# Up and gate projections as seven half-size products instead of eight, in a three-layer network on one core

## The chip, the core and the metric

One core of a Trainium2 chip runs the whole program in one launch. The metric is the device time of an execution in microseconds (us), as the median of several runs; less is better. The engines are TensorE (PE, matmuls out of SBUF into PSUM banks), VectorE (DVE), ScalarE (ACT), GpSimd (POOL) and SyncE (SP, which here issues the DMAs).

## The reference

512 tokens of width 1024, everything in fp32. The changed part is the feed-forward work of each layer:

```python
# layers 1 and 2 (first_block): D_FF = 4096
def squared_relu_mlp(x, w_up, w_down):
    return jnp.square(jax.nn.relu(x @ w_up)) @ w_down
h = layer_norm(DN_ALPHA * h + mix, ln_mix_g[i], ln_mix_b[i])
h = layer_norm(DN_ALPHA * h + squared_relu_mlp(h, mlp_w_up[i], mlp_w_down[i]), ln_mlp_g[i], ln_mlp_b[i])
# layer 3 (second_block): FFN_HIDDEN = 2816, mod = silu(c) @ w_ada + b_ada
mod = cond @ w_ada[l] + b_ada[l]
h = modulate(rms_norm(x, norm_ffn_g[l]), sh2, sc2)
ffn = (jax.nn.silu(h @ w_gate[l]) * (h @ w_up[l])) @ w_down[l]
x = x + g2[:, None, :] * ffn
return rms_norm(x, final_norm_g)
```

Ahead of each stand a mixer and its output projection (sparse attention in layer 1, gated linear attention in layer 2, attention and mLSTM in layer 3), which the change leaves as they are.

## The kernel before

Every fp32 operand of a large product is held as two parts, hi (the value rounded to fp32r) and lo (the rest), and a product is three matmuls: hi x hi, hi x lo, lo x hi (`mm3`, line 79; every matmul of that kind is recorded at line 77). The high part is a ScalarE copy (`hi`, line 87/88), the low part a subtraction (`lo`, line 84/85).

Weights stream through three rotating pairs of buffers of 1 MB (pool `wp`, `bufs=2`): `raw` takes the DMA from SP, `wh` and `wl` its parts. `wcols` (line 122) loads, `wsplit` (line 107) splits in two pieces; VectorE makes the low part of one, GpSimd that of the other. Both run under `urgent` (line 59), which gives them a priority ahead of all other work, in their own order. The framework sorts each engine's instructions by priority and readiness ahead of time; on the chip each engine then runs its list in order.

The input of an MLP lies in SBUF as `xT_hi` and `xT_lo` (features on partitions, 8 blocks of 128 features x 512 tokens). `proj_pairs` (line 185) makes blocks of 128 hidden columns x 512 tokens: 8 feature blocks x 3 matmuls of 512 columns into a PSUM bank with the tag "a" (three of them) or "o" (one). Called with two pairs, as at the start of each MLP and of the FFN, it makes four blocks and does the first 256 tokens of all before the second 256, with 256-column matmuls, so that it can begin while the last two token tiles are still being normalised.

`mlp` (line 508) works through the 4096 hidden columns in four groups of 1024: eight hidden blocks, each evacuated by ReLU on ScalarE, a square and a low part on VectorE (`ev_up`, lines 519 to 523) into `hh` and `hl`; then the down projection with these 1024 rows, for each half of the 1024 outputs, in four token tiles of 128 (`proj_tok`, `proj_steps`, line 147; 24 matmuls of 512 columns a tile). `ev` adds each tile into `acc` on VectorE (lines 534 and 536); in the last group's second half tile after tile gets its layer norm (`ln_stats`, `ln_tile`, lines 217 to 235), whose output is transposed on TensorE (line 207) and split for the next stage. In the first MLP `ada` (line 722) is interleaved: six rows of `mod`, two after each of the first three groups, each with eight loads of 512 KB (`mod_raw`, three buffers), eight VectorE operations (lines 742 and 744) and four small matmuls into a bank "s".

`ffn` (line 1155) does the same for 22 hidden blocks in groups of 8, 8 and 6: gate block through SiLU on ScalarE, up block times it on VectorE, split; in the last group the down tiles are multiplied by `g2`, added to x, normalised and written out (lines 1204 to 1217).

## Time and profile before

| | |
|---|---|
| median of 3 runs | 1968.23 us (1962.83 to 1969.54) |
| span of the profiled execution | 1965.4 us |
| TensorE busy | 1893.6 us, 8980 matmuls |
| VectorE busy | 1101.5 us |
| ScalarE busy | 770.3 us |
| GpSimd busy | 432.6 us |
| first MLP, FFN (after their first four blocks) | 293 to 633, 1614 to 1958 us |
| second MLP (after its first four blocks) | 937 to 1260 us |

A busy time says how long an engine had an instruction in it. An engine that is busy nearly all the time in a stage is that stage's first candidate for the bound; the chain of waits, followed back from the end, says which engine's work really followed on which. In the list of instructions a matmul's own duration includes its run through the array, which overlaps with the next one; what a matmul costs in a stream is the distance from start to start. The clock that TensorE was granted is given in tenths or hundredths of 2.4 GHz. All durations below come from the one profiled execution, whose time is its span.

### The profile page before, as it was taken

Reading aid. Unit: us, or ns where it says so; the run is one execution under the profiler, and the core shown is the slowest. Engines: PE = TensorE matmul, PEld = TensorE weight load, DVE = VectorE, ACT = ScalarE, POOL = GpSimd, SP = SyncE. Lnnn points to the kernel's source line nnn. Section 1 sums busy time; section 2 is a strip of 40 time slices with the busy share of each in tenths; the row PEclk is TensorE's granted clock in tenths of the full one; section 3 lists DMA queues with packets and bytes.
Section 4 is the critical chain, followed back from the end, with each engine's and each line's share of the span. In section 5 each row is a group of like instructions: output and inputs, shape, how many; then the busy total and the mean of one; then the engine's idle time right before and its main releaser. Section 6 shows DMA issues by size and latency. Waiting matters only on the chain.

```text
span 1965.4 us, 23252 instructions
## 1 busy us (share of the span) xinstructions
PE 1893.6 (96%) x8980; PEld 1506.7 (77%) x8980; DVE 1101.5 (56%) x1866; ACT 770.3 (39%) x1378; POOL 432.6 (22%) x221
## 2 busy tenths in 40 slices
PE   8999999999999999999999999999999899999998
PEld 7865688777878788778888888777666688888886
DVE  4997575657465478556533434668875762223235
ACT  5578532223232443422322323235667442223133
POOL 2121122222221212111222222312103221122621
PEclk9999999999999999999999999999999999999999
DMA  4222144556442311124233223222112132232322
GB/s 135 86 51 79 52 154 160 174 193 215 133 144 84 98 44 57 61 84 129 94 100 106 86 86 107 85 65 95 43 22 81 43 102 91 86 108 86 103 79 75
DMA packets 126106, 190.58 MB, mean 97 GB/s; under 512 B 8239, under 2 KB 76795, under 8 KB 125996
## 3 DMA queue, kind: packets, MB, share of 16 engines
q1 hardware_dynamic: 125956, 189.03, 29.8%
q8 instruction: 71, 1.16, 0.2%
q14 instruction: 39, 0.32, 0.1%
q0 software_dynamic: 32, 0.07, 0.0%
q10 hardware_dynamic: 8, 0.00, 0.0%
HBM read 186.95 MB, written 2.12 MB: 96 GB/s over the span
## 4 chain that ended last, share of the span: by engine, by line
PE 80%; DVE 11%; issue 3%; ACT 2%; DMA 2%; POOL 0%; SPq 0%; DVEq 0%; ACTq 0%; POOLq 0%
PE ps_a L77 66%; PE ps_o L77 4%; DMA mod_raw<-in_w_ada_dram 2%; PE ps_s L77 2%; DVE wl L85 2%; PE ps_t L347 2%; PE ps_t L207 1%; PE ps_s L639 1%; DVE mod_acc L744 1%; PE ps_a L1095 1%; PE ps_t L310 1%; DVE x_tok L232 1%; DVE sc L426 1%; PE ps_s L1061 1%; ACT wh L88 1%
## 5 line engine op out<-in xcount | busy, mean ns | idle before, releaser
L85 POOL TENSOR_TENSOR wl<-wr,wh 128x1024 fp32r<-128x1024 f32 (+3 forms) x145 | 368.0, 2540 | 1309.5 <-ACT wh L88 1204.1
L88 ACT ACTIVATE wh<-wr 128x1024 fp32r<-128x1024 f32 (+2 forms) x290 | 283.5, 1025 | 503.0 <-PE ps_a L77 400.2
L77 PE MATMUL ps_a<-xT_hi,wh 128*128 128x512 f32 (+1 forms) x1056 | 402.1, 381 | 0.0
L77 PE MATMUL ps_a<-xT_lo,wh 128*128 128x512 f32 (+1 forms) x1056 | 401.2, 380 | 0.0
L77 PE MATMUL ps_a<-xT_hi,wl 128*128 128x512 f32 (+1 forms) x1056 | 401.2, 380 | 0.0
L85 DVE TENSOR_TENSOR wl<-wr,wh 128x1024 fp32r<-128x1024 f32 (+3 forms) x145 | 183.1, 1263 | 328.2 <-ACT wh L88 324.9
L77 PE MATMUL ps_a<-wh,hh 128*128 128x512 f32 x688 | 269.1, 391 | 0.4 <-ACT hh L88 0.4
L77 PE MATMUL ps_a<-wh,hl 128*128 128x512 f32 x688 | 268.9, 391 | 0.2 <-DVE hl L85 0.2
L77 PEld LDWEIGHTS ps_a<-xT_hi,wh 128*128 128x128 f32 x1056 | 202.4, 192 | 41.4 <-ACT wh L88 1.2
L77 PEld LDWEIGHTS ps_a<-xT_lo,wh 128*128 128x128 f32 x1056 | 202.5, 192 | 40.4 <-issue 1.6
L77 PEld LDWEIGHTS ps_a<-xT_hi,wl 128*128 128x128 f32 x1056 | 202.1, 191 | 40.1 <-issue 0.8
L77 PE MATMUL ps_a<-wh,xT_hi 128*128 128x512 f32 (+3 forms) x536 | 208.1, 393 | 1.9 <-ACT xT_hi L88 1.9
L77 PE MATMUL ps_a<-wh,xT_lo 128*128 128x512 f32 (+3 forms) x536 | 207.4, 390 | 0.5 <-DVE xT_lo L85 0.5
L77 PE MATMUL ps_a<-wl,hh 128*128 128x512 f32 x688 | 186.1, 391 | 0.0
L77 PEld LDWEIGHTS ps_a<-wh,hh 128*128 128x128 f32 x688 | 129.2, 188 | 28.7 <-ACT hh L88 0.8
L77 PEld LDWEIGHTS ps_a<-wh,hl 128*128 128x128 f32 x688 | 129.2, 188 | 28.4 <-DVE hl L85 0.5
L77 PEld LDWEIGHTS ps_a<-wl,hh 128*128 128x128 f32 x688 | 129.0, 188 | 27.8
L77 PE MATMUL ps_a<-wl,xT_hi 128*128 128x512 f32 (+3 forms) x536 | 147.7, 386 | 0.0
L77 PEld LDWEIGHTS ps_a<-wh,xT_lo 128*128 128x128 f32 x536 | 103.4, 193 | 20.8 <-issue 1.6
L77 PEld LDWEIGHTS ps_a<-wh,xT_hi 128*128 128x128 f32 x536 | 103.5, 193 | 20.1 <-ACT xT_hi L88 2.2
L77 PEld LDWEIGHTS ps_a<-wl,xT_hi 128*128 128x128 f32 x536 | 96.4, 190 | 18.1 <-issue 0.8
L522 DVE TENSOR_TENSOR relu<-relu 128x512 f32<-128x512 f32 x64 | 87.8, 1375 | 25.2 <-ACT relu L521 25.2
(368 smaller groups left out, 2314.8 us busy)
## 6 DMA issues: line engine op xcount, KB each, us to landing
wr<-in_mlp_w_up_dram SPq DMA_DIRECT2D x32, 1024.0 KB
wr<-in_mlp_w_down_dram SPq DMA_DIRECT2D x32, 1024.0 KB
mod_raw<-in_w_ada_dram SPq DMA_DIRECT2D x48, 512.0 KB
wr<-in_b_w_in_dram SPq DMA_DIRECT2D x12, 1024.0 KB
wr<-in_w_gate_dram SPq DMA_DIRECT2D x11, 1024.0 KB
wr<-in_w_up_dram SPq DMA_DIRECT2D x11, 1024.0 KB
wr<-in_w_in_dram SPq DMA_DIRECT2D x10, 1024.0 KB
wr<-in_w_down_dram SPq DMA_DIRECT2D x10, 1024.0 KB
```

The source lines that it names most:

```text
L77: self.nc.tensor.matmul(ps, lt, rt, start=first, stop=last)
L85: (eng or self.nc.vector).tensor_tensor(out, x, hi.bitcast(F32), op=ALU.subtract)
L88: self.nc.scalar.activation(out, x, AF.Copy)
L207: self.nc.tensor.transpose(ps[:, j * P : (j + 1) * P], src[:, j * P : (j + 1) * P], self.ident)
L232: nc.vector.scalar_tensor_tensor(x, x, rs, b[:, sl], op0=ALU.mult, op1=ALU.add)
L310: nc.tensor.transpose(ps[:, j * P : (j + 1) * P], st[:, j0 + j, :], net.identr)
L347: nc.tensor.transpose(pst[:, kb * P : (kb + 1) * P], pr[:, kb * P : (kb + 1) * P], net.ident)
L426: nc.vector.scalar_tensor_tensor(sc, rl, iws[:, t, h : h + 1], sc, op0=ALU.mult, op1=ALU.add)
L522: nc.vector.tensor_tensor(r, r, r, op=ALU.mult)
L639: nc.tensor.matmul(ps[:, c * 64 : c * 64 + 64], x[:, c * C : (c + 1) * C], xv[:, c * m : (c + 1) * m, 1, :], start=True, stop=True)
L744: nc.vector.scalar_tensor_tensor(acc, raw, cd[:, k : k + 1], acc, op0=ALU.mult, op1=ALU.add)
L1061: nc.tensor.matmul(ps, qk[:, 4 + h, a * P : (a + 1) * P], qk[:, h, :], start=True, stop=True)
```

## The change

The up projection of a 256-column chunk is seen as a 2 x 2 block product: the weight chunk [1024, 256] as four quarters (two halves of the rows, two blocks of 128 columns), the input as four quarters (two halves of the features, two halves of the tokens). In Strassen's form (with the sums as Winograd arranged them) seven products of quarters do what eight did, with sums of quarters taken before and after:

- `x_sums`, once for an MLP or the FFN, makes four sums of input quarters and splits each into `th` and `tl`, on VectorE and ScalarE. Its scratch tiles have the tags "eo" (two buffers) and "eu".
- `w_sums` takes the place of `wsplit` for these chunks: parts of three raw quarters into `wh` and `wl`, four sums in place, parts of the four sums into `wsh` and `wsl` (three buffers each, two used by a chunk). All low parts and sums are VectorE's, GpSimd takes none.
- `proj_seven` runs the seven products, each of 4 feature blocks x 3 matmuls of 256 columns, two products to a PSUM bank ("aaao", all four), and combines them on VectorE into `eo`.
- The down projection takes 512 rows at a time (`down_half`) and stands between the up chunks: chunk 2g, down of group g-1, chunk 2g+1. Its tiles use the banks "s" and "t" in turn, one tile after the other.
- The first two chunks of an MLP (the first of gate and of up in the FFN) stay as one proj_pairs call with 256-column matmuls.
- In the MLPs the square moves from VectorE to ScalarE, down tiles are added into x itself, the norm's rows are loaded into the buffers of `th` and `tl` at the end; `ada` gives one row after each of six groups, with two buffers for `mod_raw`; in the FFN all scaling by `g2` moves to the last group.

The rest of the diff removes comments. Its core:

```diff
+    def x_sums(self, pool):
+        th = pool.tile([P, 4, 4, S // 2], F32R, tag="th", name="th")
+        tl = pool.tile([P, 4, 4, S // 2], F32R, tag="tl", name="tl")
+        q = lambda x, k, t: x[:, 4 * k : 4 * k + 4, t * (S // 2) : (t + 1) * (S // 2)].bitcast(F32)
+        h, l = lambda k, t: q(self.xh, k, t), lambda k, t: q(self.xl, k, t)
+        tt = nc.vector.tensor_tensor
+        tmp = pool.tile([P, 4, S // 2], F32, name="eu")
+        f3, f1 = (pool.tile([P, 4, S // 2], F32, tag="eo", name="xsum", bufs=2) for _ in range(2))
+        for f, a, b in ((f3, (1, 1), (0, 1)), (f1, (0, 0), (0, 1))):
+            tt(f, h(*a), h(*b), op=ALU.subtract)
+            tt(tmp, l(*a), l(*b), op=ALU.subtract)
+            tt(f, f, tmp, op=ALU.add)
+        self.split(th[:, 0], tl[:, 0], f1)
+        self.split(th[:, 2], tl[:, 2], f3)
+        tt(f3, f3, h(0, 0), op=ALU.add)
+        tt(f3, f3, l(0, 0), op=ALU.add)
+        nc.scalar.activation(th[:, 1], f3, AF.Copy, scale=-1.0)
+        nc.vector.scalar_tensor_tensor(tl[:, 1], f3, -1.0, th[:, 1].bitcast(F32), op0=ALU.mult, op1=ALU.subtract)
+        tt(f3, f3, h(1, 0), op=ALU.subtract)
+        tt(f3, f3, l(1, 0), op=ALU.subtract)
+        self.split(th[:, 3], tl[:, 3], f3)
+    def w_sums(self, pool, w, c0):
...
+            a11, a21, a12, a22 = v[:, 0, :, 0], v[:, 0, :, 1], v[:, 1, :, 0], v[:, 1, :, 1]
+            self.hi(q4(wh[:, 0:512]), a11)
+            self.hi(wh[:, 512:1536], raw[:, 1024:2048])
+            self.lo(q4(wl[:, 0:512]), a11, q4(wh[:, 0:512]))
+            self.lo(wl[:, 512:1536], raw[:, 1024:2048], wh[:, 512:1536])
+            tt(a22, a22, a21, op=ALU.add)
+            tt(a21, a21, a11, op=ALU.add)
+            tt(a11, a11, a22, op=ALU.add)
+            tt(a12, a12, a11, op=ALU.add)
+            for i in range(2):
+                self.hi(sh[i], v[:, i])
+                self.lo(sl[i], v[:, i], sh[i])
...
+    def proj_seven(self, pool, w, c0, xs):
...
+        b0, b1, b2, b3 = (self.bank(x) for x in "aaao")
+        prods = [("A11", raw(0, 0), b0[:, :H]), ("A12", raw(1, 0), b1[:, :H]), ("A22", ts(3), b3[:, H:]),
+                 ("S2", ts(1), b1[:, H:]), ("S1", ts(0), b2[:, :H]), ("S3", ts(2), b2[:, H:]), ("S4", raw(1, 1), b3[:, :H])]
+        for name, (xh, xl), ps in prods:
+            wh, wl = ws[name]
+            for k in range(4):
+                self.mm(ps, wh[:, k], xh[:, k], k == 0, False)
+                self.mm(ps, wh[:, k], xl[:, k], False, False)
+            for k in range(4):
+                self.mm(ps, wl[:, k], xh[:, k], False, k == 3)
+            if name == "A11":
+                nc.scalar.activation(eu[:, 3], ps, AF.Copy)
+            elif name == "S2":
+                tt(eo[:, 0], eu[:, 3], b1[:, :H], op=ALU.add)
+                tt(eu[:, 0], eu[:, 3], b1[:, H:], op=ALU.add)
+            elif name == "S3":
+                tt(eu[:, 1:3], eu[:, 0:1].to_broadcast([P, 2, H]), two(b2), op=ALU.add)
+                tt(eo[:, 3], eu[:, 2], b2[:, :H], op=ALU.add)
+        tt(eo[:, 1:3], eu[:, 1:3], two(b3), op=ALU.add)
 def mlp(net, i, extra=None, parts=True, after=None):
...
+        def up(c):
+            e = net.proj_seven(mp, w_up, c * 256, xs)
+            hh, hl = hidden()
+            for h in range(2):
+                v = e[:, 2 * h : 2 * h + 2]
+                nc.scalar.activation(v, v, AF.Relu, scale=1.0 - 2.0 * h)
+            nc.scalar.activation(e, e, AF.Square)
+            v = e.rearrange("p (f t) n -> p f (t n)", f=2)
+            net.split(hh, hl, v)
...
+        net.proj_pairs([(w_up, 2 * i * P, lambda b, ps, i=i: ev_up(2 * i + b, ps)) for i in range(2)])
+        for g in range(1, NG + 1):
+            if g < NG:
+                up(2 * g)
...
             for n in range(2):
+                down_half(net, w_dn, g - 1, n, hid, ev_dn)
+            if g < NG:
+                up(2 * g + 1)
+            if extra is not None and g <= 6:
+                extra[g - 1](mp)
 def ffn(net):
...
+        def up(c):
+            sg = net.proj_seven(fp, wg, c * 256, xs)
+            for h in range(2):
+                v = sg[:, 2 * h : 2 * h + 2]
+                nc.scalar.activation(v, v, AF.Silu, scale=1.0 - 2.0 * h)
+            e = net.proj_seven(fp, wu, c * 256, xs)
+            hh, hl = hidden()
+            nc.vector.tensor_tensor(e[:, 0:2], e[:, 0:2], sg[:, 0:2], op=ALU.mult)
+            nc.vector.scalar_tensor_tensor(e[:, 2:4], e[:, 2:4], -1.0, sg[:, 2:4], op0=ALU.mult, op1=ALU.mult)
+            net.split(hh, hl, e.rearrange("p (f t) n -> p f (t n)", f=2))
...
+        net.proj_pairs([(wg, 0, ev_g), (wu, 0, ev_u)])
+        up(1)
+        for g in range(1, NG + 1):
+            if g < NG:
+                up(2 * g)
...
             for n in range(2):
+                down_half(net, wd, g - 1, n, hid, ev_dn)
+            if 2 * g + 1 < NCH:
+                up(2 * g + 1)
```

In `mlp` NG is 8, so chunks 2 to 15 go through `proj_seven`; in `ffn` NCH is 11 and NG 6, so chunks 1 to 10, gate and up each.

## Rows read from the trace of the kernel before

**Rows 1.** The page's first part: busy time, share of the span and instructions of each engine.
```profile
PE 1893.6 (96%) x8980; PEld 1506.7 (77%) x8980; DVE 1101.5 (56%) x1866; ACT 770.3 (39%) x1378; POOL 432.6 (22%) x221
```

**Rows 2.** Busy time by stretch (first MLP, second MLP, FFN, each after its first four blocks): start and end, length, busy time and count of PE, PEld, DVE, ACT, POOL, granted clock, DMA share, GB/s.
```profile
293.00:633.00 340.00, 334.39 (x1469) 267.57 (x1468) 195.94 (x191) 93.97 (x121) 76.59 (x30) 0.99 0.48 160
...
937.00:1260.00 323.00, 323.00 (x1397) 262.38 (x1396) 131.86 (x133) 94.62 (x124) 73.36 (x29) 1.00 0.31 98
...
1614.00:1958.00 344.00, 343.95 (x1485) 278.91 (x1484) 108.03 (x112) 96.63 (x132) 96.03 (x47) 1.00 0.28 92
```

**Rows 3.** The chain that ended last, in order of time: start, length, what, number of instructions. The first row lies in the 256-column matmuls of the FFN's first pairs; the two others are 512-column streams of the second MLP and of the FFN.
```profile
936.97 322.24 PE ps_a L77 x1392
...
1601.89 8.55 PE ps_a L77 x72
...
1613.28 344.69 PE ps_a L77 x1488
```

**Rows 4.** Instructions in order of time in the FFN, by engine (VectorE, ScalarE, GpSimd): start, duration, engine, line, operation, count, idle time before.
```profile
1702.79 1.22 DVE L85 TENSOR_TENSOR wl<-wr,wh 128x1024 fp32r<-128x1024 f32 x1 [4.21 <-ACT wh L88]
...
1701.69 2.01 ACT L88 ACTIVATE wh<-wr 128x1024 fp32r<-128x1024 f32 x2 [1.26 <-PE ps_a L77]
...
1703.84 2.42 POOL L85 TENSOR_TENSOR wl<-wr,wh 128x1024 fp32r<-128x1024 f32 x1 [3.01 <-ACT wh L88]
```

**Rows 5.** Groups of instructions in the first MLP (293 to 633 us), VectorE and ScalarE, shapes kept apart: count, busy us, mean ns of one, idle before.
```profile
L744 DVE SCALAR_TENSOR_TENSOR mod_acc<-mod_raw,cond,mod_acc 128x1024 f32<-128x1024 f32 x39 | 58.4, 1498 | 10.0 <-DMA mod_raw<-in_w_ada_dram 9.5
...
L536 DVE TENSOR_TENSOR acc<-acc,ps_a 128x512 f32<-128x512 f32 x22 | 15.1, 688 | 46.8 <-PE ps_a L77 46.8
...
L756 DVE TENSOR_TENSOR mod_row<-ps_s,mod_b 128x256 f32<-128x256 f32 x6 | 2.5, 420 | 0.4 <-PE ps_s L77 0.4
...
L88 ACT ACTIVATE hh<-relu 128x512 fp32r<-128x512 f32 x29 | 18.3, 632 | 77.7 <-DVE relu L522 77.7
L521 ACT ACTIVATE relu<-ps_a 128x512 f32<-128x512 f32 x28 | 16.3, 583 | 15.9 <-PE ps_a L77 15.7
```

**Rows 6.** VectorE in order of time: the last low parts of xT ahead of the first MLP, the second MLP and the FFN.
```profile
276.32 1.37 DVE L85 TENSOR_TENSOR xT_lo<-ps_t,xT_hi 128x512 fp32r<-128x512 f32 x2 [1.85 <-ACT xT_hi L88]
...
920.47 1.36 DVE L85 TENSOR_TENSOR xT_lo<-ps_t,xT_hi 128x512 fp32r<-128x512 f32 x2 [2.20 <-ACT xT_hi L88]
...
1599.59 0.69 DVE L85 TENSOR_TENSOR xT_lo<-ps_t,xT_hi 128x512 fp32r<-128x512 f32 x1 [0.58 <-ACT xT_hi L88]
```

**Rows 7.** The chain that ended last: the last of the four first blocks (bank "o") in the first MLP, the second MLP and the FFN.
```profile
289.98 2.85 PE ps_o L77 x24
...
934.12 2.85 PE ps_o L77 x24
...
1610.43 2.85 PE ps_o L77 x24
```

**Rows 8.** TensorE's matmuls in order of time around 263 to 271 us, the start of the first MLP.
```profile
262.66 0.28 PE L77 MATMUL ps_a<-xT_hi,wl 128*128 128x256 f32 x1
...
265.08 0.36 PE L77 MATMUL ps_a<-xT_hi,wh 128*128 128x256 f32 x1
...
268.56 0.41 PE L77 MATMUL ps_a<-xT_hi,wl 128*128 128x256 f32 x1
...
268.78 0.41 PE L77 MATMUL ps_a<-xT_hi,wh 128*128 128x256 f32 x1
...
270.91 0.32 PE L77 MATMUL ps_a<-xT_lo,wh 128*128 128x256 f32 x1
...
271.07 0.28 PE L77 MATMUL ps_a<-xT_hi,wl 128*128 128x256 f32 x1
...
271.19 0.28 PE L77 MATMUL ps_a<-xT_hi,wh 128*128 128x256 f32 x1
```

**Rows 9.** VectorE in order of time at the end of the first MLP (first operation of each of the four last token tiles, then the last operation) and of the second (first and last).
```profile
622.08 0.69 DVE L536 TENSOR_TENSOR acc<-acc,ps_a 128x512 f32<-128x512 f32 x1 [3.07 <-PE ps_a L77]
...
628.93 0.68 DVE L536 TENSOR_TENSOR acc<-acc,ps_a 128x512 f32<-128x512 f32 x1
...
635.47 0.68 DVE L536 TENSOR_TENSOR acc<-acc,ps_a 128x512 f32<-128x512 f32 x1
...
647.76 0.68 DVE L536 TENSOR_TENSOR acc<-acc,ps_a 128x512 f32<-128x512 f32 x1
...
654.69 1.37 DVE L85 TENSOR_TENSOR xT_lo<-ps_t,xT_hi 128x512 fp32r<-128x512 f32 x2 [1.80 <-ACT xT_hi L88]
...
1253.73 0.69 DVE L536 TENSOR_TENSOR acc<-acc,ps_a 128x512 f32<-128x512 f32 x1 [3.06 <-PE ps_a L77]
...
1295.99 1.29 DVE L85 TENSOR_TENSOR xT_lo<-ps_t,xT_hi 128x512 fp32r<-128x512 f32 x2 [0.84 <-ACT xT_hi L88]
```

**Rows 10.** Busy time by stretch, columns as in rows 2: the end of the first MLP with the start of layer 2, and the worst 10 us at the end of the second MLP.
```profile
633.00:671.00 38.00, 34.30 (x245) 32.59 (x246) 21.13 (x27) 12.10 (x19) 11.64 (x7) 0.91 0.24 71
...
1270.00:1280.00 10.00, 5.87 (x25) 4.66 (x24) 9.63 (x9) 3.01 (x6) 5.68 (x2) 0.90 0.43 127
```

**Rows 11.** VectorE in order of time: the last token tile of the FFN.
```profile
1957.99 0.69 DVE L1204 TENSOR_TENSOR acc<-ps_a,g 128x512 f32<-128x512 f32 x1 [0.20 <-PE ps_a L77]
1958.71 0.69 DVE L1205 TENSOR_TENSOR x_tok<-x_tok,acc 128x512 f32<-128x512 f32 x1
1959.44 0.69 DVE L1208 TENSOR_TENSOR acc<-x_tok,gf 128x512 f32<-128x512 f32 x1
1960.25 0.16 DVE L782 TENSOR_TENSOR sd<-fsq 128x1 f32<-128x1 f32 x1
1960.77 0.16 DVE L785 RECIPROCAL rs<-sd 128x1 f32<-128x1 f32 x1 [0.36 <-ACT sd L783]
1960.97 0.49 DVE L1216 TENSOR_SCALAR acc<-acc,rs 128x512 f32<-128x512 f32 x1
```

**Rows 12.** Who waited for whom on TensorE in the first MLP (total us, times, longest us), and SP's queue in order of time at that MLP's start.
```profile
PE ps_s L77 <- DVE mod_acc L744: 5.0, 3, 2.0
...
275.72 10.35 SPq L740 DMA_DIRECT2D mod_raw<-in_w_ada_dram  x5
```

**Rows 13.** GpSimd and VectorE in order of time: two GpSimd low parts, the two VectorE operations that ran beside them, and the same two VectorE operations with GpSimd idle.
```profile
638.96 5.74 POOL L85 TENSOR_TENSOR wl<-wr,wh 128x1024 fp32r<-128x1024 f32 x2 [18.29 <-ACT wh L88]
...
639.81 5.43 DVE L232 SCALAR_TENSOR_TENSOR x_tok<-x_tok,rs,ln_b 128x512 f32<-128x512 f32 x2
...
632.01 1.41 DVE L232 SCALAR_TENSOR_TENSOR x_tok<-x_tok,rs,ln_b 128x512 f32<-128x512 f32 x2
```

More of the change, by code (lines that the diff above doesn't have):

```diff
@@ L145, in proj_tok, with proj_steps @@
             pass
-    def proj_steps(self, ah, al, chunks, n, evac, tiles=range(NT), serial=False):
+    def proj_steps(self, ah, al, chunks, n, evac, tiles=range(NT), serial=False, tags="a"):
         tiles = list(tiles)
@@ L160, in proj_steps @@
                     if ci == 0:
-                        ps[t] = self.bank("a")
+                        ps[t] = self.bank(tags[t % len(tags)])
                     ts = slice(t * P, (t + 1) * P)
@@ new lines, in mlp, with hidden, ev_up @@
+        xs = net.x_sums(mp)
+        hid, ln = [], []
+        NG = 8
+        def hidden():
+            hid.append([mp.tile([P, 2, S], F32R, tag=x, name=x, bufs=3) for x in ("hh", "hl")])
+            return hid[-1]
+        def ev_up(j, ps):
+            hh, hl = hidden() if j % 2 == 0 else hid[-1]
+            r = mp.tile([P, S], F32, tag="eo", name="relu", bufs=2)
+            nc.scalar.activation(r, ps, AF.Relu)
+            nc.vector.tensor_tensor(r, r, r, op=ALU.mult)
+            net.split(hh[:, j % 2, :], hl[:, j % 2, :], r)
@@ L738, in piece @@
         for k in range(KB):
-            raw = pool.tile([P, D], F32, name="mod_raw", bufs=3)
+            raw = pool.tile([P, D], F32, name="mod_raw", bufs=2)
             nc.sync.dma_start(raw, w[k * P : (k + 1) * P, cg * D : (cg + 1) * D])
@@ new lines, in ffn, with hidden, ev_g, ev_u @@
+        xs = net.x_sums(fp)
+        hid, rows = [], []
+        NCH = 11
+        NG = 6
+        def hidden():
+            hid.append([fp.tile([P, 2, S], F32R, tag=x, name=x, bufs=3) for x in ("hh", "hl")])
+            return hid[-1]
+        gate = []
+        def ev_g(j, ps):
+            if j == 0:
+                gate.append(fp.tile([P, 2, S], F32, tag="eo", name="silu", bufs=2))
+            nc.scalar.activation(gate[0][:, j, :], ps, AF.Silu)
+        def ev_u(j, ps):
+            hh, hl = hidden() if j == 0 else hid[-1]
+            s = gate[0][:, j, :]
+            nc.vector.tensor_tensor(s, s, ps, op=ALU.mult)
+            net.split(hh[:, j, :], hl[:, j, :], s)
@@ new lines, in ev_dn @@
+        def ev_dn(g, n, t, ps):
+            sl = slice(n * 512, (n + 1) * 512)
+            o, x = acc[:, t, sl], net.xt[:, t, sl]
+            if g == 0:
+                nc.scalar.activation(o, ps, AF.Copy)
+                return
+            nc.vector.tensor_tensor(o, o, ps, op=ALU.add)
+            if g < NG - 1:
+                return
+            g2, gf = rows
+            nc.vector.tensor_tensor(o, o, g2[:, sl], op=ALU.mult)
+            nc.vector.tensor_tensor(x, x, o, op=ALU.add)
+            junk = fp.tile([P, 512], F32, tag="eo", name="junk", bufs=2)
+            nc.scalar.activation(junk, x, AF.Square, accum_out=sq[:, t, n : n + 1])
+            nc.vector.tensor_tensor(o, x, gf[:, sl], op=ALU.mult)
+            if n == 1:
+                rs = rms_rstd(net, sq[:, t, :])
+                for q in range(2):
+                    x = acc[:, t, q * 512 : (q + 1) * 512]
+                    if q == 0:
+                        nc.scalar.activation(x, x, AF.Copy, scale=rs)
+                    else:
+                        nc.vector.tensor_scalar(x, x, rs, None, op0=ALU.mult)
+                    nc.sync.dma_start(net.out[0, t * P : (t + 1) * P, q * 512 : (q + 1) * 512], x)
@@ new lines, in ffn @@
+        net.proj_pairs([(wg, 0, ev_g), (wu, 0, ev_u)])
[3 more added lines that the diff above has]
+                up(2 * g)
+            else:
+                for tag, row in (("th", net.mod[5]), ("tl", I["final_norm_g_2"])):
+                    rows.append(fp.tile([P, D], F32, tag=tag, name="row_" + tag))
+                    net.bcast_row(rows[-1], row)
+            for n in range(2):
+                down_half(net, wd, g - 1, n, hid, ev_dn)
+            if 2 * g + 1 < NCH:
+                up(2 * g + 1)
```

134 lines of the change are left out of this document (49 added, 85 removed).

## The prediction

> **What bounds the kernel now.** I read the totals first: TensorE is busy for 1893.6 us of the 1965.4 us span [rows 1]. Then the stages, for an average hides them: in the first MLP TensorE works 334.4 of 340 us, in the second 323.0 of 323, in the FFN 343.95 of 344, while VectorE has 196, 132 and 108 us of work there [rows 2]. So in the three stretches that the change touches the path is the matmul stream itself, and the chain of waits says the same: it runs through 1392 and 1488 matmuls without a break [rows 3]. Two things are worth reading: what a matmul costs at either width, and how much of VectorE's time is free exactly where the new work falls.
>
> **What the change takes away.** 1488 matmuls of 512 columns take 344.69 us, 231.6 ns each; 72 of 256 columns take 8.55 us, 118.8 ns each [rows 3]. A chunk of 256 hidden columns is now 2 blocks x 8 x 3 = 48 wide matmuls, 11.12 us; as seven products it is 7 x 12 = 84 narrow ones, 9.98 us. Each MLP keeps its first two chunks (a four-block proj_pairs) and converts 14: 155.6 - 139.7 = 15.9 us. The FFN converts 10 chunks of gate and up: 222.3 - 199.6 = 22.8 us. Sum **-54.6 us**. The down products keep their number and width.
>
> **What one chunk costs VectorE.** Alone, a 128x1024 subtraction takes 1.22 us, ScalarE's two copies of that size 2.01, GpSimd's subtraction 2.42 [rows 4]; a 512-wide VectorE operation takes 0.69, a 256-wide one on PSUM 0.42 [rows 5]. The seven-product form needs, all on VectorE: low parts 0.69 + 1.22 + 2 x 1.22, four sums 4 x 0.69, together 7.1 us before the products; 3 x 0.42 + 2 x 0.69 = 2.6 us to combine them; 1.22 for the hidden low part. That is 11.0 us beside 9.98 us of TensorE, where it has about 4 us per chunk today, as GpSimd makes half of the low parts and nothing is combined. With the downs in between (two chunks and two downs: 19.9 + 22.2 = 42.2 us of TensorE; 21.9 + 2.4 + 8 x 0.69 = 29.9 us of VectorE) the mean still fits. What counts is where VectorE's work has a date.
>
> **Starts of the three stretches: +40.** x_sums has 14 VectorE operations of 1024 elements, 17.2 us, and all wait for the last token tile. x is complete at 277.7, 921.8 and 1600.3 [rows 6]; the first pairs end at 292.8, 937.0 and 1613.3 [rows 7]: cover of 15.1, 15.1 and 13.0 us. But the third product (A22) wants the sum that is made last, the first chunk's w_sums (7.1 us, urgent, so ahead of x_sums) falls into the same time, and the two x_sums scratch tiles hold both "eo" buffers, in which the ReLU of the first four blocks must land before its PSUM banks come free; the fourth bank is A22's. Laid end to end for an MLP: 17.2 + 7.1 + 1.2 (next down's low part) + a chain of about 2.7 (multiply 0.69, copy 0.63, low part 0.69, ReLU 0.58 [rows 5]) = 28.2 us after x, 32 if the sums also wait for ScalarE three times and for the port. A22 would be due 15.1 + 2.9 = 18.0 after x: 10 to 14 us late, I take 12. Bound below: x_sums first, only A22's own low parts before it: 17.2 + 1.9 + 2.7 = 21.8, 4 us. In the FFN the up weights' sums (5.9 us) are urgent too and the cover is 2 us shorter: 14 to 18, I take 16; bound below 4.
>
> **The clock after such a gap: +4.** After the 5 us near 263 in which TensorE nearly stood, 256-column matmuls start 0.21 us apart (1.2 GHz) until 270.9, then 0.12 (2.4 GHz) [rows 8]: 2.4 us at half speed, 1.2 lost. Three starts: 4; between 0 and 6.
>
> **The last down of each MLP: +8.4.** Today eight blocks stand in a group, so the last block's evacuation hides behind the others. Now the last chunk is followed by its own down: combine 0.69, ReLU 2 x 0.58, square 1.0, high part 1.0, low part 1.22 [rows 4, 5], with the hand-overs some 5.3 us, of which 1.1 us of matmuls hide: 4.2 each. The other downs are one chunk late, so their evacuation has 10 us; the FFN's last down has an older group before it.
>
> **Ends: +30.** A last down tile now takes 12 matmuls, 2.78 us, not 24, 5.56. The layer norm behind it is VectorE work that no longer fits: tiles begin at 622.1, 628.9, 635.5 and 647.8 and end at 656.1 in the first MLP, and run from 1253.7 to 1297.3 in the second [rows 9], 34 and 43.5 us for work that TensorE releases over 22. TensorE has idle time there already (34.3 of 38 us busy; 5.87 of 10 in the worst stretch) [rows 10]. The chain begins 2.8 us earlier after that half's first matmul, but TensorE has 11.1 us less to do beside it: 8.3 us each. In the FFN the last group has 2 blocks, 1.39 us a tile; VectorE needs four operations (0.72 apart) a tile, 2.9, and 0.8 more in the second half for the scale [rows 11]: 4 x 2.9 + 4 x 3.7 = 26 us from 1.4 us on, against 11.1 of matmuls. The tail after the last matmul is 7.4 us now (1957.97 [rows 3] to 1965.4) and becomes 1.4 + 26 + 0.8 + 3.9 - 11.1 = 21: +13. The cover that hid this is the longer last group.
>
> **Inside the groups: +16.** Weight buffers allow one chunk ahead. Where two chunks touch in an MLP, VectorE has 7.1 + 2.6 + 0.7 (last down tile) = 10.4 us due in 9.98; the urgent sums go ahead of the combination that frees the next A22's bank. 12 times 0 to 1.5, I take 0.5: 6. In the FFN four chunks touch: 3 x 7.1 + 3 x 2.6 + 2.7 + 1.2 = 33 us due in 29.9 and the last fifth of the run: 0 to 5, I take 2.5, in four runs (the first is in the start): 10.
>
> **The ada rows in the first MLP: +5.** A row is one first operation and seven multiply-adds of 1.5 us [rows 5], 12 us with its ends. With a group's 29.9 that is 42 of 42.2 us, and the GpSimd halves take more: VectorE beside a GpSimd part needed 5.43 us for a pair of operations that takes 1.41 alone [rows 13]. Two buffers instead of three for mod_raw mean that SP, which already stands 10.35 us at five such loads, waits in front of the weight loads. TensorE waited 5.0 us for these rows [rows 12]; six groups at -1 to +5 each, I take 10, less those 5.0: +5, between -5 and +25.
>
> The Trainium skill, "SBUF — State Buffer", section "Who interferes with whom", says that a VectorE instruction with two SBUF inputs and a GpSimd one that reads SBUF exclude each other and that the second fully blocks; [rows 13] agree. By it the chunks, which leave GpSimd out, would lose no time to the port and the groups would stand at their lower bound: the sum would be 16 us less.
>
> **Sum.** -54.6 + 40 + 4 + 8.4 + 30 + 16 + 5 = +48.8 on a span of 1965.4, which lies 2.8 below the median of 1968.23. On the median's scale: **2017 us**. All unknown terms at their lower ends: -54.6 + 12 + 0 + 8.4 + 30 + 0 - 5 = -9, 1959; at their upper ends +98, 2066.
>
> **Rivals.**
> The busiest engine decides: TensorE is busy 96% and VectorE 56% of the span [rows 1], the means per group fit, so VectorE's additions vanish in its idle time. It would cost nothing but the unhidden chain at two MLP ends, 1968.2 - 54.6 + 8.4 = **1922**, and up to 1957 with parts of the starts and ends. Against it: work with a date, 17.2 us in 13 to 15 of cover, and ends where VectorE is the bound already. 0.10. The Trainium skill, "Perfetto Trace Analysis", section "Identifying the Most-Contended Engine", names the engine of highest occupancy as the one to relieve first; taken alone that gives this rival.
> The sums are made in the order of need: starts 4 us each, groups free, only the ends remain: 1958 to 1974, middle **1965**, no change. It decides whether x_sums goes ahead of the weights' sums. 0.10.
> The forecast, VectorE's dated work takes more than TensorE gives back: 1974 to 2050, **2017**. It decides from 55 us of new waits on; ends and chains alone are 38. 0.72.
> VectorE is the bound all through: ada groups +25, 5 us in each FFN run, **2060**. 0.07.
> Narrow matmuls don't run at half price, as each loads its weights anew: at 231.6 ns, 4032 x 0.113 = +455 on the forecast, 2472. Against it: the 118.8 ns are of a stream that loads each time [rows 3]. 0.01.
>
> **How the numbers follow.** The likeliest case gives 2017. From 1957 to 2050 the range holds the second and third cases, 0.82. A measurement here tells 0.3% (6 us) from nothing: faster is the first case and a third of the second, 0.13; within 0.3% is what is left of the second and the lowest edge of the third, 0.08; slower the rest, 0.79.
>
> **What would show it.** Narrow matmuls 0.119 us apart, and 4032 more of them for 2304 fewer wide ones; TensorE idle 10 to 16 us before the third product of the first chunk, with VectorE full and x_sums ending late; a gap of 4 us at each MLP's last down; some 21 us after the last matmul; VectorE over 80% busy in all three stretches. It is wrong if TensorE stays above 95% through the starts and ends: then the lists of VectorE are hidden after all.

## The result, and the profile after

The changed kernel takes 1989.86 us (median of 4 runs, 1985.63 to 1992.29), the kernel before 1967.47 us beside it: a ratio of 1.0116, 95% interval 1.0095 to 1.0137. The forecast was 2017 us. It had the direction right and the size more than twice too large: +49 us forecast, +22.4 measured. The profiled execution has a span of 1988.7 us, 23.3 more than the one before, and the steps are settled against that number.

The page's first part (busy time, share, instructions), to be held against [rows 1]:

```profile
PE 1859.5 (94%) x10708; PEld 1559.6 (78%) x10708; DVE 1471.0 (74%) x2486; ACT 897.0 (45%) x1524; POOL 307.9 (15%) x157
```

TensorE is busy 34 us less and VectorE 370 us more. The same three stretches as in [rows 2], and 75 us at the start of the FFN:

```profile
293.00:675.00 382.00, 355.51 (x2174) 312.85 (x2174) 304.43 (x383) 147.30 (x185) 59.35 (x22) 0.97 0.48 155
941.00:1255.00 314.00, 307.58 (x1903) 274.82 (x1901) 222.12 (x280) 136.75 (x166) 50.85 (x16) 0.99 0.32 104
1614.00:1972.00 358.00, 341.77 (x2323) 314.50 (x2321) 273.41 (x369) 136.79 (x178) 27.39 (x12) 0.99 0.28 89
...
1604.00:1679.00 75.00, 63.84 (x494) 62.27 (x495) 66.23 (x86) 33.90 (x45) 4.12 (x2) 0.93 0.27 85
```

VectorE (the third busy time) went from 196, 132 and 108 us to 304, 222 and 273, and TensorE, which had filled the last two and all but 6 us of the first, now has holes: 26, 6 and 16 us. Of the chain that ended last, narrow products of one chunk of the second MLP (A11 and A12, and S2, S1 and S3 behind A22, which is not in these rows); below them TensorE's waits over the whole span (engine, line, waited for: total us, times, longest):

```profile
1068.09 2.85 PE ps_a L77 x24
...
1072.36 4.32 PE ps_a L77 x36
```

```profile
PE ps_t L301 <- DVE hm L921: 16.0, 4, 6.1
PE ps_o L77 <- DVE eo L293: 14.9, 11, 2.3
PE ps_t L301 <- DVE x_tok L326: 13.5, 6, 4.0
PE ps_s L77 <- DVE hl L85: 10.5, 7, 3.6
PE ps_o L77 <- DVE silu L1300: 6.1, 1, 6.1
```

With A22 these are six products of 12 matmuls each, from 1068.09 to 1076.68 us: 8.59 us, 0.119 for a matmul of 256 columns, and the gain is there, to within some 2 us in all. It is eaten in three kinds of places that this list names: at the ends of the MLPs (`hm`, `x_tok`: transposes that wait for the layer norm), at the joins of chunks (`eo`: A22 waits until the chunk before it leaves bank o), and at the starts (`hl`, `silu`).

To put a number on each place I took the starts of all matmuls in the trace and summed, by place, what lies between two of them beyond the stream's own step (0.2315 us behind 512 columns, 0.1188 behind 256; the first row of the table is the forecast's, at these steps). This counts half-speed matmuls after a gap as well, and an entry is good to about 1 us. After less before, in us:

| place | first MLP | second MLP | FFN | sum | forecast |
|---|---|---|---|---|---|
| narrow products | -15.9 | -15.9 | -22.8 | -54.6 | -54.6 |
| start, with the clock | 12.9 | 5.7 | 11.6 | 30.2 | 44 |
| groups, with the ada rows | 4.5 | 4.1 | 10.2 | 18.8 | 21 |
| last down and end of the MLP | 6.3 | 13.3 | | 19.6 | 25 |
| FFN after the last matmul | | | 9.0 | 9.0 | 13 |

The sum is +23.0, and the spans differ by 23.3. Every loss is where the forecast put it and all are smaller, the starts most of all. What the table can't say is why each is there. That is what the experiments ask.

### The profile page after: what moved, and what is told of

Its sections match the earlier page's. It is cut to its first block, busy times and chain, and to the rows that moved or that the text cites. A ratio compares the mean times of both kernels' runs of the same rounds, so it can differ in the third digit from the quotient of the medians.

```text
span 1988.7 us, 27371 instructions
## 1 busy us (share of the span) xinstructions
PE 1859.5 (94%) x10708; PEld 1559.6 (78%) x10708; DVE 1471.0 (74%) x2486; ACT 897.0 (45%) x1524; POOL 307.9 (15%) x157
## 4 chain that ended last, share of the span: by engine, by line
PE 62%; DVE 23%; issue 5%; DMA 5%; ACT 5%; POOL 1%; SPq 0%; DVEq 0%; ACTq 0%; POOLq 0%
PE ps_a L77 27%; PE ps_s L77 10%; PE ps_t L77 9%; PE ps_o L77 8%; DVE wl L85 4%; DMA mod_raw<-in_w_ada_dram 2%; DVE wsl L85 2%; DMA wr<-in_mlp_w_down_dram 2%; ACT wh L88 2%; PE ps_t L441 2%; PE ps_t L301 1%; PE ps_s L759 1%; DVE mod_acc L864 1%; DVE hl L85 1%; PE ps_a L1215 1%
## 5 line engine op out<-in xcount | busy, mean ns | idle before, releaser
L77 PE MATMUL ps_a<-xT_hi,wh 128*128 128x256 f32 (+1 forms) x672 | 193.7, 307 | 2.1 <-DVE eu L289 1.3
L77 PE MATMUL ps_a<-xT_lo,wh 128*128 128x256 f32 (+1 forms) x672 | 192.1, 304 | 0.0
L77 PE MATMUL ps_a<-xT_hi,wl 128*128 128x256 f32 (+1 forms) x672 | 157.4, 304 | 0.0
L77 PE MATMUL ps_s<-wh,hl 128*128 128x512 f32 x344 | 137.2, 399 | 10.7 <-DVE hl L85 10.5
L77 PE MATMUL ps_a<-th,wsh 128*128 128x256 f32 x576 | 145.8, 284 | 1.5 <-ACT silu L1295 1.3
L77 PE MATMUL ps_a<-tl,wsh 128*128 128x256 f32 x576 | 145.4, 284 | 0.0
L77 PE MATMUL ps_s<-wh,hh 128*128 128x512 f32 x344 | 136.1, 396 | 5.0 <-ACT hh L88 5.0
L77 PE MATMUL ps_t<-wh,hh 128*128 128x512 f32 x344 | 137.4, 399 | 0.6 <-DVE xT_lo L85 0.6
L77 PE MATMUL ps_t<-wh,hl 128*128 128x512 f32 x344 | 137.1, 398 | 0.0
L85 DVE TENSOR_TENSOR wsl<-wr,wsh 128x1024 fp32r<-128x1024 f32 x96 | 126.1, 1326 | 0.6 <-ACT wsh L88 0.4
```

Of the source, the lines that this page charges most:

```text
L77: self.nc.tensor.matmul(ps, lt, rt, start=first, stop=last)
L85: (eng or self.nc.vector).tensor_tensor(out, x, hi.bitcast(F32), op=ALU.subtract)
```

## The experiments

What the first four expectations call theory A is the reading of this table: each loss sits at its own place, goes with what the forecast named as its cause there, and comes back in full once that is taken away. The rival that grew out of e1 and e4, and is tried from e5 on: TensorE runs one list in order, and what is lost depends on which product stands where in it and on which bank it writes, more than on how much VectorE has to do.

**e1_ends.** The last down group of each MLP and of the FFN is made three chunks long (the group before it gives up a chunk in the MLPs and falls away in the FFN), which should give the ends their cover back.

```diff
-                down_half(net, w_dn, g - 1, n, hid, ev_dn)
+            c0, m = (2 * g - 3, 3) if g == NG else (2 * g - 2, 1) if g == NG - 1 else (2 * g - 2, 2)
+                down_half(net, w_dn, g - 1, c0, m, n, hid, ev_dn)
 ...
-            for n in range(2):
-                down_half(net, wd, g - 1, n, hid, ev_dn)
+            c0, m = (2 * g - 4, 3) if g == NG else (2 * g - 2, 2)
+            for n in range(2 if g != NG - 1 else 0):
+                down_half(net, wd, g - 1, c0, m, n, hid, ev_dn)
```

> The last down group of each stage has three chunks instead of two (MLP) or one (FFN), so a last token tile takes 18 matmuls, 4.2 us, in place of 12 (2.8 us) or 6 (1.4 us). Theory A (VectorE's chains at the three ends are late because the last downs became short): the FFN's tail after its last matmul falls from 16.9 us to about 8, and each MLP's end gets some 4 us shorter; span 1988.7 - 9 - 2 x 4 = about 1972, ratio to the kernel before 1.003. Rival B (the time went into the narrow matmul stream and the starts; the ends only move work that TensorE does anyway): under 3 us of change, span about 1986.

Measured: 1993.94 us, ratio 1.013 (1.0107 to 1.0152): no gain. The FFN's tail, from the end of the last matmul on, did shrink from 16.4 to 9.1 us, but the first MLP became 4 us longer and the second about 10, with the wait for `hm` up from 16.0 us in 4 places:

```profile
PE ps_t L301 <- DVE hm L922: 23.3, 5, 8.7
```

So the forecast's mechanism, cover, and with it theory A, holds for the FFN and not for the MLPs: there TensorE has three chunks' worth of down tiles to do, and waits all the same. Something else holds them.

**e2_no_xsums.** The VectorE operations of x_sums are replaced by ScalarE copies, so that the sums of x are left out.

```diff
-        for f, a, b in ((f3, (1, 1), (0, 1)), (f1, (0, 0), (0, 1))):
-            tt(f, h(*a), h(*b), op=ALU.subtract)
...
+        for i, a in enumerate(((0, 0), (0, 1), (1, 0), (1, 1))):
+            nc.scalar.activation(th[:, i], h(*a), AF.Copy)
+            nc.scalar.activation(tl[:, i], l(*a), AF.Copy)
```

> x_sums leaves out its fourteen VectorE operations: the parts of the four sums are plain ScalarE copies of input quarters, so the products are those of other numbers. Theory A (x_sums is late work at the three starts): TensorE's waits in the first 30 us of each stage go away, about 5 us in the second MLP, 8 in the FFN, 5 to 10 in the first MLP; span 1966 to 1971. Rival B (the weights' sums and combinations of the chunks are what is late at the starts): at most 4 us in all, span above 1984.

Measured: 1972.59 us in one run (span 1970.8, 18 us less). The three sets of sums cost 18 us together, 6 a stretch, not 12 to 16. By the starts of matmuls, the second MLP's start loses 0.1 us instead of 5.7, so there the sums of x are all of it; the first MLP's loses 5.8 instead of 12.9, and the FFN's about half of its 11.6. TensorE's wait for `silu` is gone from the list too.

**e3_ada_one_load.** Each ada row is made from one of its eight loads and multiply-adds; seven are left out.

```diff
-        for k in range(KB):
+        for k in range(1):
```

> Each ada row takes one of its eight loads and multiply-adds, so the modulation rows are sums over an eighth of the width. Theory A (VectorE is full in the first MLP because of the rows): the six waits of 1 to 2.4 us for the bank of the third product there, 9.4 us in all, shrink to the second MLP's 0.5, and the waits of 5 us near 314 to 322 behind a mod_raw load go too: the first MLP takes 14 to 18 us less, span about 1972. Rival B (the bank is late by the form of the chunk itself): the six waits stay above 6 us, and only the 5 us at the start go.

Measured: 1973.07 us in one run (span 1971.3, 17 us less); layer 2 begins 20.2 us earlier. With the rows nearly gone, the first MLP loses 6.1 us at its start and 3 in its groups, instead of 12.9 and 15 (here not less the before, which loses about 10 in its groups). At that start the rows are as dear as the sums of x, and in the groups they cost 12 us more.

**e4_a22_later.** A22, the product that needs both the last sum of x and bank o, goes from third to fifth.

```diff
-        prods = [("A11", ...), ("A12", ...), ("A22", ts(3), b3[:, H:]),
-                 ("S2", ...), ("S1", ...), ("S3", ...), ("S4", ...)]
+        prods = [("A11", ...), ("A12", ...), ("S2", ...),
+                 ("S1", ...), ("A22", ts(3), b3[:, H:]), ("S3", ...), ("S4", ...)]
```

> Product A22 is fifth instead of third in a chunk, which gives VectorE 2.9 us more to free its bank from the chunk before; nothing else changes. Theory A (where two chunks touch, TensorE waits for that bank alone): the waits for bank o, 8.4 us in the first MLP and 6.5 in the FFN, go, and 6 of the FFN's start: span 1988.7 - 15 to 20 = 1969 to 1974. Rival B (VectorE is short of time there, the wait only shows where): the waits move to the next product or bank, less than 6 us won, span above 1983.

Measured: 1961.84 us, ratio 0.9972 (0.9962 to 0.9982), 28 us less than the kernel as changed (26 by the spans) and 0.3% below the kernel before, with every operation still there. The waits for `eo`, 14.9 us in 11 places, are gone from the list; the sum of lost time in the groups falls from 15 to 3 us in the first MLP and from about 10 to nothing in the FFN. VectorE has as much to do as in the kernel as changed, so its amount of work alone did not make the joins dear: with A22 later the same work fits. In the first MLP either cure does, as e3 had brought the same 15 us to 3 by taking work from VectorE.

**e5_end_banks.** On top of e4: the last down tiles of each MLP take banks a and s in turn instead of s and t.

```diff
-def down_half(net, w, g, n, hid, evac, serial=False):
+def down_half(net, w, g, n, hid, evac, tags="st"):
 ...
-                 lambda t, ps: evac(g, n, t, ps), serial=True, tags="st")
+                 lambda t, ps: evac(g, n, t, ps), serial=True, tags=tags)
 ...
-                down_half(net, w_dn, g - 1, n, hid, ev_dn)
+                down_half(net, w_dn, g - 1, n, hid, ev_dn, "as" if g == NG else "st")
```

> The kernel of e4_a22_later (span 1962.4 us) with one more edit: the last down tiles of each MLP alternate between banks a and s instead of s and t. Bank theory: the transposes of the finished layer norm take bank t in TensorE's list, and two of the four last down tiles stand behind them in the same two buffers; in the trace of after the second ps_t tile reached VectorE at 1279.8 although TensorE could have run it at about 1267, and TensorE waited 16 us for hm and 13.5 us for x_tok. Freed of that, each MLP end should lose about 5 us less: about 1952 us, and those two waits together below 20 us. Theory of the forecast (the layer norm on VectorE no longer fits beside the short downs, 8.3 us an end): the banks make no difference, 1959 to 1965 us.

Measured: 1944.54 us, ratio 0.9876 (0.986 to 0.9893), 17 us less than e4 by the medians and 21 by the spans, twice what I had expected.

**e9_banks_alone.** The same bank edit, on the kernel as it was changed.

> The changed kernel as it was given, with the bank edit of e5_end_banks alone (last down tiles of each MLP in banks a and s; A22 still third). If the shared bank t is what the ends of the MLPs cost, and that is independent of the place of A22, the same 21 us come off: about 1968 us, no difference from before. If e5's gain came only with A22 moved: above 1978 us.

Measured: 1971.42 us, ratio to before 1.0019 (1.001 to 1.0028): 18.4 us less than the kernel as changed by the medians, 20.9 by the spans. One shared bank is worth nearly all that the change lost on balance, and about a quarter of the 77.9 us (23.3 and 54.6) that went into waits; e4's order is worth as much again. By the starts of the same instructions in both traces, 6.7 us are gone when the second MLP begins and 20.5 when the FFN does, and the FFN itself gains nothing: this is all that the table puts at the two ends. The trace shows how. VectorE's evacuations of the second half's four last down tiles, at the end of the second MLP, in the changed kernel:

```profile
1264.48 0.69 DVE L646 TENSOR_TENSOR x_tok<-x_tok,ps_s 128x512 f32<-128x512 f32 x1 [0.32 <-PE ps_s L77]
...
1268.89 0.68 DVE L646 TENSOR_TENSOR x_tok<-x_tok,ps_s 128x512 f32<-128x512 f32 x1
...
1279.76 0.69 DVE L646 TENSOR_TENSOR x_tok<-x_tok,ps_t 128x512 f32<-128x512 f32 x1 [3.17 <-PE ps_t L77]
...
1299.89 0.69 DVE L646 TENSOR_TENSOR x_tok<-x_tok,ps_t 128x512 f32<-128x512 f32 x1 [2.52 <-PE ps_t L77]
```

and in e9_banks_alone:

```profile
1253.44 0.67 DVE L646 TENSOR_TENSOR x_tok<-x_tok,ps_a 128x512 f32<-128x512 f32 x1
...
1257.84 0.68 DVE L646 TENSOR_TENSOR x_tok<-x_tok,ps_s 128x512 f32<-128x512 f32 x1
1258.44 0.68 DVE L646 TENSOR_TENSOR x_tok<-x_tok,ps_a 128x512 f32<-128x512 f32 x1
...
1263.61 0.63 DVE L646 TENSOR_TENSOR x_tok<-x_tok,ps_s 128x512 f32<-128x512 f32 x1
```

Four tiles in 35 us there, in 10 us here. TensorE's list in the changed kernel says what lies between (start, duration, idle before):

```profile
1272.99 2.24 PE L301 MATMUL ps_t<-ident,hm 128*128 128x128 f32 x8 [5.80 <-DVE hm L921]
...
1275.51 0.80 PE L77 MATMUL ps_t<-wh,hh 128*128 128x512 f32 x1
...
1288.43 1.94 PE L301 MATMUL ps_t<-ident,hm 128*128 128x128 f32 x8 [6.15 <-DVE hm L921]
```

The transposes of the finished tile write bank t too. The third down tile in that order, whose operands had long been there, stands behind them at 1275.5; they wait 5.8 us for `hm`; and when the third and fourth tiles are done at last, little is left on TensorE to hide their layer norms. It also explains e1, where the same two tiles begin right behind transposes again:

```profile
1277.05 0.79 PE L77 MATMUL ps_t<-wh,hh 128*128 128x512 f32 x1 [0.29 <-DVE xT_lo L85]
...
1300.25 0.79 PE L77 MATMUL ps_t<-wh,hh 128*128 128x512 f32 x1 [0.56 <-DVE xT_lo L85]
```

More matmuls per tile don't help if the tile is held behind a transpose. Tag a also has three buffers where t has two; that this counts beside the sharing is not ruled out by a run, but what stands ahead of the two tiles in the list is the transposes.

**e6_x_sums_first.** The sums of x in the urgent order, ahead of the weight sums.

```diff
-        xs = net.x_sums(mp)
+        with net.urgent():
+            xs = net.x_sums(mp)
```

> The changed kernel with one edit: the sums of x stand in the urgent order, ahead of the weight sums of the first chunk. The forecast's second rival (order of need decides; starts cost 4 us each instead of 12 to 16): about 28 us less than after, some 1961 us. My present theory: the starts lost only about 26 us in all, part of it in the ada rows and the clock, since TensorE's list had other products and the first down ahead of A22; the weights' parts now come some 17 us later and the first products of the chunk wait instead: 1980 to 1992 us.

Measured: 1986.14 us, one run, 4 less than the kernel as changed and inside the spread of its runs. TensorE's wait for `eo` stays, and a new one comes for `wsh`, the weights' sums:

```profile
PE ps_o L77 <- DVE eo L293: 13.2, 10, 2.3
PE ps_a L77 <- ACT wsh L88: 9.5, 5, 3.5
```

So far as one run and this form of it tell, the forecast's second rival, order of need, falls: what a start wins in sums, it pays in weights.

**e7_ffn_tail.** On top of e4: the FFN's last down group three chunks long, the MLPs as they were (e1's FFN lines with constants).

> The kernel of e4_a22_later (span 1962.4 us) with the last down group of the FFN of three chunks instead of one, so that 33 us of matmuls lie beside the last evacuations instead of 11. Cover theory (the forecast's step on the tail): the stretch after the last matmul shrinks from 16.8 to about 9 us and nothing else moves: about 1954 us. Rival, from e1_ends, where the tail shrank to 9.4 us but the kernel was 4 us slower: the longer group costs as much in front of the last matmul as it saves behind it: 1960 to 1964 us.

Measured: 1955.91 us, ratio 0.9933 (0.9914 to 0.9952), span 8.7 less than e4. The last two matmuls of e7, where the span is 1953.7:

```profile
1943.81 0.63 PE L77 MATMUL ps_t<-wl,hh 128*128 128x512 f32 x2
```

From the end of this row the tail is 9.3 us, where e4 has 16.4. Cover, the forecast's reason, is shown for the FFN.

**e8_ada_one_group_later.** On top of e4: each ada row written one group later.

```diff
-            if extra is not None and g <= 6:
-                extra[g - 1](mp)
+            if extra is not None and 2 <= g <= 7:
+                extra[g - 2](mp)
```

> The kernel of e4_a22_later (span 1962.4 us) with the six ada rows one group later in the first MLP (groups 2 to 7 instead of 1 to 6), so that no row falls into the start of the first MLP. If the row is what makes the first MLP's start the dearest (VectorE stands in front of its loads, TensorE works 44 of 53 us between 277 and 330): 5 to 8 us less, about 1956 us. If the start is bound by the sums of x themselves: no change, 1960 to 1965 us. If group 7 has no room for a row: the end of the first MLP pays, 1965 us or more.

Measured: 1963.49 us, ratio 0.9965 (0.9952 to 0.9979), no different from e4. But the trace says that the trial wasn't made (the first operation of the rows there; count, shortest, median and longest in ns, first and last start):

```profile
L862 DVE TENSOR_SCALAR mod_acc<-mod_raw,cond x2: 739/742/745, 282.9 to 394.1; 128x1024 f32<-128x1024 f32 x2
```

The first row still begins at 282.9 us, in the start (283.0 in e4), as the framework sorts by readiness too. An order in the text is no order on the engine.

**e13_row_after_start and e14_row_after_start_given.** So the first row was tied by data: a zero made from the hidden blocks of the second chunk of seven products (chunk 3) is added to its condition. e13 stands on e12 (below), e14 on the kernel as changed.

```diff
-                extra[g - 1](mp)
+                extra[g - 1](mp, hid[2 * g + 1][0][:, 0, 0:1].bitcast(F32))
 ...
-            nc.scalar.activation(cd, cd, AF.Silu)
+            zero = pool.tile([P, 1], F32, name="zero")
+            nc.vector.tensor_scalar(zero, after, 0.0, None, op0=ALU.mult)
+            nc.scalar.activation(cd, cd, AF.Silu, bias=zero)
```

> The kernel of e12_ffn_multiply_first (span 1933.9 us) with the first ada row tied to the hidden blocks of the second chunk (a zero made from them is added to the condition), so that no row can run in the start of the first MLP. In e8 the row was only written later, and the trace shows it at 282.9 us all the same. Starts of matmuls further apart than the stream's own step add up to 13 us in that start. If the row in VectorE's list is the cause (a part of it behind its loads): about 7 us less there, some 1928 us on the profiled span. If the sums of x alone are the cause: no change, 1932 to 1936. If the six rows no longer fit behind it: more.

> The changed kernel as it was given (span 1988.7 us), with the same tie of the first ada row and nothing else. If the row is half of what the first MLP's start costs here too: 5 to 8 us less, about 1982 us. If the groups, which have no slack with A22 third, lose what the start wins: no change.

Measured: 1950.05 us (ratio 0.9912, 0.9893 to 0.9931), 12 more than e12; and 1997.69 (1.015, 1.0125 to 1.0174), 8 more than the kernel as changed. Now the row is out of the start, and TensorE's busy time in the first MLP's start shows it, first in the changed kernel, then in e13 (e12 has 66.48):

```profile
266.00:341.00 75.00, 64.71 (x407) 58.75 (x408) 66.16 (x79) 28.76 (x39) 14.31 (x3) 0.93 0.45 146
...
266.00:341.00 75.00, 70.59 (x470) 65.36 (x471) 65.51 (x82) 31.96 (x40) 15.38 (x4) 0.95 0.32 101
```

By starts of matmuls, the start loses 5.7 instead of 13 us. But the row's own matmul then finds its sums late:

```profile
372.27 1.08 PE L77 MATMUL ps_s<-mod_acc,ones 128*32 128x256 f32 x8 [9.12 <-DVE mod_acc L867]
```

9 us in one place, and the groups together lose about 20 us more than in e12. Of the first MLP's start, about 7 us are the ada row and 6 the sums of x; the row is better off there.

**e10_all_three.** The edits of e4, e5 and e7 together.

> A22 fifth, last down tiles of the MLPs in banks a and s, last down group of the FFN of three chunks: the edits of e4, e5 and e7 together. They act at different places, so the sum should hold: 1944.5 less 6 to 9, that is about 1936 us, a ratio of 0.982 to 0.985 to before. If the pieces trade against each other: 1942 us or more.

Measured: 1939.61 us, ratio 0.9861 (0.9847 to 0.9876), span 1936.2. From e5 it is 4.9 us by the medians and 4.8 by the spans, where e7 alone gave 5.9 and 8.7.

**e11_gpsimd_low_part.** On top of e10: one low part of each chunk on GpSimd.

```diff
-            self.lo(wl[:, 512:1536], raw[:, 1024:2048], wh[:, 512:1536])
+            self.lo(wl[:, 512:1536], raw[:, 1024:2048], wh[:, 512:1536], nc.gpsimd)
```

> The kernel of e10_all_three with one of VectorE's low parts of every chunk (128x1024, start to start 1.13 us) given to GpSimd. If VectorE's amount of work still sets the pace inside the groups: 34 x 1.1 us lighter on VectorE, 5 to 10 us less than e10. If VectorE and GpSimd get in each other's way as in rows 13, or the low part is late there (2.4 us and more): 3 to 15 us more than e10. If the groups have slack by now: no change.

Measured: 1957.4 us, ratio 0.9946 (0.9929 to 0.9963), 18 more than e10. VectorE has less work and the kernel is slower. Two groups of VectorE's operations in the FFN (count, busy us, mean ns, idle before), in e11 (1660 to 1925 us) and then in the same stretch of e10 (1640 to 1905 us), say why:

```profile
L85 DVE TENSOR_TENSOR wsl<-wr,wsh 128x1024 fp32r<-128x1024 f32 x32 | 56.5, 1776 | 7.5 <-ACT wsh L88 7.4
...
L250 DVE TENSOR_TENSOR wr<-wr 128x512 f32<-128x512 f32 x16 | 11.0, 685 | 16.4 <-POOL wl L85 16.4
```

```profile
L85 DVE TENSOR_TENSOR wsl<-wr,wsh 128x1024 fp32r<-128x1024 f32 x32 | 44.9, 1415 | 0.5 <-ACT wsh L88 0.4
...
L250 DVE TENSOR_TENSOR wr<-wr 128x512 f32<-128x512 f32 x16 | 11.0, 689 | 0.3
```

The sums are made in place, so the first one waits until GpSimd has read the raw weights, 1.0 us a chunk, with VectorE's whole list behind it; and VectorE's subtractions beside GpSimd's get longer, 11.6 us in all. The second is what [rows 13] showed; the Trainium skill, "SBUF — State Buffer", section "Who interferes with whom", has it as a lock on a shared port, with which the 361 ns more of a mean subtraction agree. The first was a new wait. How the 18 us divide between the two no run shows.

**e12_ffn_multiply_first.** On top of e10: in the FFN's start the multiply that frees bank o goes ahead of the up weights' sums.

```diff
-            nc.vector.tensor_tensor(s, s, ps, op=ALU.mult)
+            with net.urgent():
+                nc.vector.tensor_tensor(s, s, ps, op=ALU.mult)
```

> The kernel of e10_all_three with the multiply that frees bank o in the FFN's start put in the urgent order, ahead of the up weights' sums. In the trace of e5_end_banks A22 waits 6.1 us for that multiply at 1607.6, and the sum of x that A22 needs is ready at about 1605: the wait should fall to about 3.5 us and the time by 2 to 3 us. If what it displaces (the up weights' sums) is late in its place: no change.

Measured: 1938.41 us, ratio 0.9854 (0.984 to 0.9869), span 2.3 less than e10: as expected on the spans, but the intervals overlap and the runs can't tell it from e10. It is the fastest version that ran, 1.5% under the kernel before and 2.6% under the change as given.

## Why the prediction was wrong, step by step

The forecast was 25 us too dear on the span (+48.8 for +23.3): 14 of them at the starts, 9 at the ends and the tail, 2 in the groups.

**Narrow products, -54.6.** Right: 0.119 us each, and the count is that of the page, 10708 matmuls for 8980. The rival of full price falls.

**Starts and clock, +44: the step that failed most, by 14 us.** The mechanism is there: VectorE is busy 66 of 75 us in the FFN's and in the first MLP's start, and A22 came late, in the first MLP at 309.78 us, where "18.0 after x" made it due at about 296. So "10 to 14 us late" was right. But I charged all of the delay to the path. The first product with a sum and the first down run ahead of it, in TensorE's order:

```profile
297.44 0.50 PE L77 MATMUL ps_s<-wh,hh 128*128 128x512 f32 x1 [3.02 <-ACT hh L88]
...
301.38 0.41 PE L77 MATMUL ps_a<-th,wsh 128*128 128x256 f32 x1
...
309.78 0.28 PE L77 MATMUL ps_o<-th,wh 128*128 128x256 f32 x1
```

The framework sorts by priority and readiness ahead of time, as the description of the kernel before says; I used that for VectorE and forgot it for TensorE. In the first MLP the lost time then came from a term that I had put elsewhere: e13 and e3 show 7 of the 13 us to be the first ada row. In the changed kernel VectorE stands before one of its loads, with the low part that frees TensorE's next matmul behind it:

```profile
315.68 1.28 DVE L864 SCALAR_TENSOR_TENSOR mod_acc<-mod_raw,cond,mod_acc 128x1024 f32<-128x1024 f32 x1 [4.36 <-DMA mod_raw<-in_w_ada_dram]
...
318.76 0.69 PE L77 MATMUL ps_s<-wh,hl 128*128 128x512 f32 x1 [3.58 <-DVE hl L85]
```

In the FFN the 6.1 us wait ends with the multiply that frees bank o, the fourth bank, which I had named only for the ReLU of the MLPs. That multiply stood behind the sums of x in VectorE's list, as the wait is gone in e2; put ahead of the weights' sums in e12, it saves only 2 us, for A22 then waits for its sum.

**VectorE's prices** were about a tenth too high, in all terms. I took durations, 0.69 and 1.22 us; operations that don't need each other overlap. From the FFN's start in e5:

```profile
1589.38 1.21 DVE L224 TENSOR_TENSOR xsum<-xsum,xT_lo 128x1024 f32<-128x1024 f32 x1
1590.52 0.68 DVE L251 TENSOR_TENSOR wr<-wr 128x512 f32<-128x512 f32 x1
1591.12 0.68 DVE L1300 TENSOR_TENSOR silu<-silu,ps_a 128x512 f32<-128x512 f32 x1
1591.72 0.68 DVE L252 TENSOR_TENSOR wr<-wr 128x512 f32<-128x512 f32 x1
```

1.14 and 0.60 from start to start. A chunk's 11.0 us become about 10.

**Last down of each MLP, +8.4.** Too large: TensorE waits about 0.6 us at each, as its list begins the tiles of the first half with the chunk that is already there. **MLP ends, +16.6: the step that failed in its mechanism.** With the last downs 25 forecast, 19.6 measured: nearly right in size, by luck, for the cause is wrong. I had VectorE's layer norm outrun its cover; e1 gave cover and won nothing, e9 changed one bank tag of two and won 18 to 21 us, all that the ends had lost. So the direction of my forecast is partly luck too: without this loss, which I had for another reason, the kernel comes within 0.2% of the one before (e9, 1.0019). The bank is in the diff (`tags="st"`) and the transposes take bank t in the code of before; I read the diff for work and not for buffers.

**FFN tail, +13.** Mechanism right (e7), size 9.0: the operations of different tiles alternate there, at 0.60 from start to start, not 0.72.

**Groups +16 and ada +5.** 18.8 for 21. Right in size, and right that the bank of the next A22 comes free too late. But I took VectorE's 10.4 us due in 9.98 for the reason: with the same work and A22 two places later (e4) nearly all of it is gone.

**The rivals.** The busiest engine decides (1922): not in the kernel as changed, where 23.3 + 54.6 = 77.9 us went into waits; e12 comes within 16 us of it. The Trainium skill, "Perfetto Trace Analysis", section "Identifying the Most-Contended Engine", has the engine of highest occupancy improved first and judges TensorE by MFU and the busy share of its weight loads. By that share too it is TensorE here, 77% before and 78% after, against VectorE's 56 and 74%. Read as this rival reads it, as a call to take work from TensorE, the runs disagree: with 54.6 us of matmuls less the kernel is 22 us slower, and 48 us came back with TensorE's work unchanged. VectorE as the bound all through (2060) falls with e4 and e5, which leave VectorE its work and take 48 us off. What stays open: what the half of the FFN's 11.6 us at its start that is not the sums of x (e2) consists of, and how the groups could be given room for the first ada row (e13).

## What to carry to other kernels

A late operand costs what stands behind it in the waiting engine's list, not its lateness: look for what can run ahead, and put the product that needs the last operand or the scarcest bank later (fifth of seven, here). When a change gives an operation another buffer, ask who else writes that buffer, and whether that one waits for something slow; here one tag in place of another was worth some 20 us, about what the change lost on balance. Price chains by durations and independent runs of operations by their distance from start to start.

## What I had not expected of the hardware

VectorE starts an independent operation about 0.08 us before the one ahead of it has ended in the records: 0.60 us apart for 0.68 us of duration, 1.14 for 1.21. And a program order is a weak tool: moving the ada rows a group later in the text left the first one where it was (282.9 us), whereas a data dependence moved it, for a worse result.
